# HGRN2's lower bounds of the second layer, formed by channels in the first layer and loaded back in one broadcast

## The chip, the cores and the metric

The program runs on one core of a Trainium2 chip. The metric is device time in microseconds (us), the median of several executions; lower is better. The engines are named as in the profile: PE is TensorE's matmul stream, PEld its weight loads, DVE is VectorE, ACT is ScalarE, POOL is GpSimd, SP is SyncE. SPq and ACTq are the DMA queues that SP and ACT feed.

## The reference

Two layers of a hybrid model over 256 tokens of width 1024. In each layer one projection feeds four mixers of 256 channels each: HGRN2, GLA, RWKV-7 and RetNet. Their outputs go together through an output projection, a residual and a layer norm (LN1). The first layer then has a dense FFN, the second a mixture of eight experts (MoE).

The part that matters here is HGRN2's forget gate. Its lower bound is a softmax over the layers of a 2 x 256 table, summed up and taken relative to the first layer. So it is 0 in layer 0, and in layer 1 it is one number per channel:

```python
lb_all = jnp.cumsum(jax.nn.softmax(hgrn_lb_logits, axis=0), axis=0)
lb_all = lb_all - lb_all[:1]
...
f = lb + (1.0 - lb) * jax.nn.sigmoid(f_raw)          # lb = lb_all[l]
o = _chunked_gated_linear(silu(q), 1.0 - f, i, log(f))
o = _rms_norm(o, norm_g) * silu(g)
```

## The kernel before, in words

Everything is float32. A weight tile is loaded by SP into one of three `raw` buffers. ACT rounds it to its high part (`wH`), DVE forms the rest (`wL`), and PE multiplies with three matmuls per product (line 146). Names that begin with `Pws` and `Pas` are the accumulators of the input projection, `XT` is the layer's input, `YT` the input of the output projection.

Each layer runs RWKV-7 first, then RetNet, HGRN2 and GLA (`ORDER` is "rhg"). The pieces of the input projection that the later mixers need are jobs: they are interleaved with the small matmuls of the mixers (`between`, line 308) so that PE has work while a mixer waits for DVE, ACT or POOL. A scheduler then sets the order of the instructions on each engine; each engine runs its own in that order. The y of HGRN2 and of GLA (`y_late`, line 729) is transposed inside the output projection, whose parts run in the order (6, 4, 0, 2), so those of HGRN2 and GLA are the last two. The layer norm's first matmuls are called `bank_o`.

HGRN2's chain in `hgrn` (lines 673 to 718) is: three activations of the gate's input (`hg_e`, `hg_s`, `hg_e`), the lower bounds, the product and the sum with them on `hg_e` (lines 702 and 703), the logarithm `hg_lf` (line 704), its split `hs_lfH` and `hs_lfL`, matmuls with constants (`Phs_ps`), exponentials `hg_E`, score matmuls (`Phs_p1p`), masked copies into `lin_S`, the output (`Ppo`), the norm and `y_late`. In layer 0 there are no lower bounds. In layer 1 both rows of the logits are loaded as broadcasts to all 128 partitions (`bcast`, line 393, on ACT's queue), and the softmax is computed on 128 x 256 tiles: the same 256 numbers on every partition (lines 686 to 701).

A second copy of the program (`general`) stands behind a branch at the end and is not taken with these inputs.

Of the kernel before, what the change touches and what calls it, by code (L numbers as in the profile page):

```python
# [9 lines left out]
F32 = mybir.dt.float32  # L10
# [3 lines left out]
AF = mybir.ActivationFunctionType  # L14
OP = mybir.AluOpType
# [109 lines left out]
class Build:  # L125
# [547 lines left out]
    def hgrn(self, l, xf, qT, V, G):  # L673
        nc, I, c, p = self.nc, self.I, self.c, self.mp
        xf = xf()
        e = self.t2([128, 2, 256], n="hg_e")
        s = self.t2([128, 2, 256], n="hg_s")
        self.act(e, xf, AF.Exp, scale=-1.0)
        self.act(s, e, AF.Ln, bias=1.0)
        self.act(e, s, AF.Exp, scale=-1.0)  # L680
        lf = self.t2([128, 2, 256], n="hg_lf")
        kt = self.t2([128, 2, 256], n="hg_kt")
        if l == 0:
            self.ts(lf, s, -1.0, None, OP.mult)
        else:
            b0 = self.bcast(self.t2([128, 256], n="hg_b0"), I["hgrn_lb_logits"][0])
            b1 = self.bcast(self.t2([128, 256], n="hg_b1"), I["hgrn_lb_logits"][1])
            m = self.t2([128, 256], n="hg_m")
            self.tt(m, b0, b1, OP.max)
            self.tt(b0, b0, m, OP.subtract)  # L690
            self.tt(b1, b1, m, OP.subtract)
            self.act(b0, b0, AF.Exp)
            self.act(b1, b1, AF.Exp)
            self.tt(m, b0, b1, OP.add)
            nc.vector.reciprocal(m, m)
            self.tt(b0, b0, m, OP.mult)
            self.tt(b1, b1, m, OP.mult)
            self.tt(b1, b0, b1, OP.add)
            self.tt(b1, b1, b0, OP.subtract)
            om = self.t2([128, 256], n="hg_om")  # L700
            self.ts(om, b1, -1.0, 1.0, OP.mult, OP.add)
            self.tt(e, e, om[:, None, :].to_broadcast([128, 2, 256]), OP.mult)
            self.tt(e, e, b1[:, None, :].to_broadcast([128, 2, 256]), OP.add)
            self.act(lf, e, AF.Ln)
        self.ts(kt, e, -0.5, 0.5, OP.mult, OP.add)
        kT = self.t2([128, 2, T], n="hg_kT")
        ps = self.mx("Phg_ps1")
        for a in range(2):
            for tt in range(2):
                self.tr(ps[:, a * 256 + tt * 128:a * 256 + tt * 128 + 128], kt[:, tt, a * 128:(a + 1) * 128], self.ident)  # L710
        self.act(kT, ps.rearrange("p (a t) -> p a t", a=2))
        o = self.t2([128, 2, 256], n="hg_o")
        if self.general:
            self.gated_linear(2, qT(), kT, lf, V(), o)
        else:
            self.hgrn_scores(l, qT, kT, lf, V, o)
        self.dump(f"hgrn_o{l}", o)
        self.gated_norm(o, I["hgrn_norm_g"][l], G(), 0)

    def gated_norm(self, o, g, G, ct):  # L720

        ng = self.bcast(self.t2([128, 64], n="gn_ng"), g)
        self.ts(ng, ng, 0.5, None, OP.mult, eng=self.nc.gpsimd)
        v = o.rearrange("p t (h v) -> p (t h) v", v=64)
        gv = G.rearrange("p t (h v) -> p (t h) v", v=64)
        self.tt(gv, gv, ng[:, None, :].to_broadcast([128, 8, 64]), OP.mult, self.nc.gpsimd)
        self.head_norm(v, 1e-6, False, "gn")
        if ct in LATE:
            o = self.lp.tile([128, 2, 256], F32, name="y_late")
        self.tt(o.rearrange("p t (h v) -> p (t h) v", v=64), v, gv, OP.mult)  # L730
        if ct in LATE:
            self.tails[ct] = lambda: self.put_y(o, ct)
        else:
            self.put_y(o, ct)
# [925 lines left out]
```

## Time and profile before

| | |
|---|---|
| median of 3 runs | 1102.84 us (1101.68 to 1105.39) |
| profiled execution, its own time | 1104.21 us |
| its span in the trace | 1102.7 us |
| mean granted clock of PE | 0.971 |
| PE busy | 1045.3 us (95%) |
| DVE busy | 792.8 us (72%) |
| ACT busy | 617.1 us (56%) |
| POOL busy | 67.5 us (6%) |

The profiled execution is 1.4 us above the median, and 1.5 us of it lie outside the span. Times of the trace are counted from the span's start. PE is busy nearly throughout, but the granted clock is below 1 in some stretches, and a matmul at the lower clock counts as busy for longer. So busy time alone does not tell what bounds a stage. Layer 0's mixers run from 0 to about 218 us, its FFN follows, layer 1's mixers end near 641 us, and the MoE fills the rest.

### The profile page before, as it was taken

How to read it: one execution, taken by the hardware profiler on the slowest of the kernel's cores; microseconds unless marked ns; L12 is line 12 of the kernel's file. 1: busy time of each engine (PE TensorE's matmuls, PEld its weight loads, DVE VectorE, ACT ScalarE, POOL GpSimd, SP SyncE). 2: the span in 40 equal slices, each digit the busy share in tenths (PEclk: the TensorE clock that was granted, in tenths of full speed). 3: DMA queues.
4: the chain of work that ended last, by engine and by line, in shares of the span. 5: the costliest groups of instructions: out<-in, count | busy, mean ns of one | idle time of the engine just before them, and what ended most of it. 6: DMA issues, size and time to landing. Idle time of an engine off the chain costs nothing. (4 is left out here: it accounts for less than half of the span.)

```text
span 1102.7 us, 17027 instructions
## 1 busy us (share of the span) xinstructions
PE 1045.3 (95%) x6664; PEld 906.6 (82%) x6664; DVE 792.8 (72%) x1171; ACT 617.1 (56%) x871; POOL 67.5 (6%) x92
## 2 busy tenths in 40 slices
PE   7799989999999999899899899999999999999995
PEld 6788878799999888888787677888888888877883
DVE  4584675565656456685673577998999899989986
ACT  4534264345555343633363435787788778777763
POOL 2000021100000002000102140000000000010001
PEclk9899998999999999999987999999999999999998
DMA  9244244336567363343151194998899889988952
GB/s 302 87 111 126 72 154 155 116 110 188 178 189 254 139 209 124 108 116 123 48 183 49 49 362 135 356 381 297 317 353 359 310 307 362 353 274 314 363 192 79
DMA packets 142161, 228.83 MB, mean 208 GB/s; under 512 B 17604, under 2 KB 89848, under 8 KB 142072
## 3 DMA queue, kind: packets, MB, share of 16 engines
q1 hardware_dynamic: 135104, 219.76, 58.4%
q10 hardware_dynamic: 6968, 7.90, 2.2%
q8 instruction: 54, 0.88, 0.3%
q14 instruction: 35, 0.29, 0.1%
HBM read 224.50 MB, written 3.15 MB: 206 GB/s over the span
## 5 line engine op out<-in xcount | busy, mean ns | idle before, releaser
L136 DVE TENSOR_TENSOR wL<-raw,wH 128x1024 fp32r<-128x1024 f32 (+2 forms) x477 | 501.6, 1065 | 164.6 <-ACT wH L133 157.8
L133 ACT ACTIVATE wH<-raw 128x1024 fp32r<-128x1024 f32 (+2 forms) x481 | 442.1, 927 | 272.5 <-PE Pws_ps L146 94.8
L146 PE MATMUL Pws_ps<-XT,wH 128*128 128x256 f32 (+1 forms) x1248 | 234.1, 288 | 9.1 <-DVE rc_x L143 8.3
L146 PE MATMUL Pms_ps<-wH,e_X 128*128 128x512 f32 (+1 forms) x768 | 226.9, 374 | 0.0
L146 PEld LDWEIGHTS Pws_ps<-XT,wH 128*128 128x128 f32 (+1 forms) x1248 | 196.4, 192 | 13.1 <-DVE rc_x L143 9.3
L146 PE MATMUL Pws_ps<-XT,wL 128*128 128x256 f32 (+1 forms) x624 | 178.3, 286 | 0.1
L146 PEld LDWEIGHTS Pms_ps<-wH,e_X 128*128 128x128 f32 x768 | 142.1, 188 | 20.2
L146 PE MATMUL Pms_ps<-wL,e_X 128*128 128x512 f32 (+1 forms) x384 | 144.1, 375 | 1.7 <-DVE wL L136 1.7
L146 PEld LDWEIGHTS Pws_ps<-XT,wL 128*128 128x128 f32 (+1 forms) x624 | 119.7, 192 | 1.1 <-issue 0.3
L146 PE MATMUL bank_dn<-wH,e_aT 128*128 128x512 f32 x352 | 112.9, 398 | 0.3
L146 PE MATMUL Pas_ps<-wH,XT 128*128 128x256 f32 x448 | 96.1, 302 | 4.6 <-ACT p_v L133 3.2
L146 PEld LDWEIGHTS Pas_ps<-wH,XT 128*128 128x128 f32 x448 | 75.8, 200 | 9.8 <-ACT p_v L133 4.5
L146 PEld LDWEIGHTS Pms_ps<-wL,e_X 128*128 128x128 f32 x384 | 72.2, 188 | 13.4 <-DVE wL L136 2.4
L146 PEld LDWEIGHTS bank_dn<-wH,e_aT 128*128 128x128 f32 x352 | 66.0, 188 | 17.2 <-DVE e_X L136 1.6
L146 PE MATMUL bank_dn<-wL,e_aT 128*128 128x512 f32 x176 | 69.8, 396 | 0.0
L146 PE MATMUL Pas_ps<-wL,XT 128*128 128x256 f32 x224 | 67.5, 302 | 0.6 <-DVE wL L136 0.5
L146 PEld LDWEIGHTS Pas_ps<-wL,XT 128*128 128x128 f32 x224 | 44.7, 200 | 3.9 <-DVE wL L136 2.4
L146 PEld LDWEIGHTS bank_dn<-wL,e_aT 128*128 128x128 f32 x176 | 33.1, 188 | 7.6
L146 PE MATMUL bank_acc<-wH,ffn_a 128*128 128x512 f32 x88 | 33.5, 394 | 0.0
L146 PE MATMUL bank_r<-wH,ffn_a 128*128 128x512 f32 x88 | 33.3, 392 | 0.0
L146 PE MATMUL bank_acc<-wH,YT 128*128 128x512 f32 x64 | 26.3, 446 | 1.2 <-ACT YT L133 1.2
L133 ACT ACT_TABLE_LOAD x19 | 24.4, 1283 | 1.6 <-PEq L1647 1.2
(385 smaller groups left out, 1238.1 us busy)
## 6 DMA issues: line engine op xcount, KB each, us to landing
raw<-in_moe_w_down SPq DMA_DIRECT2D x40, 1024.0 KB
raw<-in_moe_w_gate SPq DMA_DIRECT2D x32, 1024.0 KB
raw<-in_moe_w_up SPq DMA_DIRECT2D x32, 1024.0 KB
raw<-in_w_in SPq DMA_DIRECT2D x29, 1024.0 KB
raw<-in_moe_w_gate SPq DMA_DIRECT2D x16, 768.0 KB
raw<-in_moe_w_up SPq DMA_DIRECT2D x16, 768.0 KB
raw<-in_ffn_w_gate SPq DMA_DIRECT2D x11, 1024.0 KB
raw<-in_ffn_w_up SPq DMA_DIRECT2D x11, 1024.0 KB
```

The costliest lines, as they stand in the source:

```text
L133: return self.nc.scalar.activation(out=out, in_=in_, func=func, **k)
L136: return (eng or self.nc.vector).tensor_tensor(out=out, in0=a, in1=b, op=op)
L146: return self.nc.tensor.matmul(out=out, lhsT=lhsT, rhs=rhs, start=start, stop=stop)
```

## The change

The softmax moves to layer 0, into a new function that is called between HGRN2's scores and its norm. It works by channels: 256 channels lie as 128 partitions x 2, so a row of logits is a tile of 128 x 2. Two loads bring the logits (element by element), eight DVE operations and one ACT exponential of 2 or 4 elements per partition form `lb_x` (the bound, and 1 minus it), and two small DMAs on SP's queue write it to DRAM (`lbd`, 2 x 256). In layer 1 one broadcast load on ACT's queue brings both rows to all partitions (`hg_lb`). The product, the sum and the logarithm stay. The branch `general` keeps the old form.

```diff
@@ hgrn
         if l == 0:
             self.ts(lf, s, -1.0, None, OP.mult)
+        elif not self.general:
+            lb = self.t2([128, 2, 256], n="hg_lb")
+            nc.scalar.dma_start(lb, self.lbd.rearrange("(o x) c -> o x c", o=1).to_broadcast([128, 2, 256]))
+            b1, om = lb[:, 0, :], lb[:, 1, :]
+            self.tt(e, e, om[:, None, :].to_broadcast([128, 2, 256]), OP.mult)
+            self.tt(e, e, b1[:, None, :].to_broadcast([128, 2, 256]), OP.add)
+            self.act(lf, e, AF.Ln)
         else:
             b0 = self.bcast(self.t2([128, 256], n="hg_b0"), I["hgrn_lb_logits"][0])
...
         self.dump(f"hgrn_o{l}", o)
+        if l == 0 and not self.general:
+            self.lower_bounds()
         self.gated_norm(o, I["hgrn_norm_g"][l], G(), 0)
+
+    def lower_bounds(self):
+
+        nc, p = self.nc, self.lp
+        b, x, m = (p.tile([128, 2, 2], F32, name="lb_" + k) for k in "bxm")
+        for l in range(2):
+            nc.scalar.dma_start(b[:, l, :], self.I["hgrn_lb_logits"][l].rearrange("(a p) -> p a", p=128))
+        self.tt(m[:, 0], b[:, 0], b[:, 1], OP.max)
+        self.tt(b, b, m[:, 0:1].to_broadcast([128, 2, 2]), OP.subtract)
+        self.act(b, b, AF.Exp)
+        self.tt(m[:, 0], b[:, 0], b[:, 1], OP.add)
+        nc.vector.reciprocal(m[:, 0], m[:, 0])
+        self.tt(b, b, m[:, 0:1].to_broadcast([128, 2, 2]), OP.mult)
+        self.tt(m[:, 1], b[:, 0], b[:, 1], OP.add)
+        self.tt(x[:, 0], m[:, 1], b[:, 0], OP.subtract)
+        self.ts(x[:, 1], x[:, 0], -1.0, 1.0, OP.mult, OP.add)
+        self.lbd = self.dp.tile([2, 256], F32, name="lbd")
+        for i in range(2):
+            nc.sync.dma_start(self.lbd[i].rearrange("(a p) -> p a", p=128), x[:, i, :])
```

The scheduler moves instructions with it. Three places matter.

**DVE in layer 1, up to the sum on `hg_e`.** Before, the reciprocal, four more operations on the bounds and `hg_om` stand in front of the product, with pieces of weights (`wL`) between them (the rows begin at the reciprocal; the first `hg_m` is nine rows further up, right behind the row `YT<-Ppy_ps`):

```order
L695 RECIPROCAL hg_m<-hg_m 128x256
L143 SCALAR_TENSOR_TENSOR p_g<-p_g,Pas_ps_5886 128x256
L136 TENSOR_TENSOR hg_b_5785<-hg_b_5785,hg_m 128x256
L136 TENSOR_TENSOR hg_b_5787<-hg_b_5787,hg_m 128x256
L136 TENSOR_TENSOR wL<-raw,wH 128x768
L136 TENSOR_TENSOR hg_b_5787<-hg_b_5785,hg_b_5787 128x256
L136 TENSOR_TENSOR wL<-raw,wH 128x768
L136 TENSOR_TENSOR hg_b_5787<-hg_b_5787,hg_b_5785 128x256
L136 TENSOR_TENSOR wL<-raw,wH 128x512
L140 TENSOR_SCALAR hg_om<-hg_b_5787 128x256
L136 TENSOR_TENSOR hg_e<-hg_e,hg_om 128x512
L136 TENSOR_TENSOR hg_e<-hg_e,hg_b_5787 128x512
```

Now:

```order
L136 TENSOR_TENSOR YT<-Ppy_ps_5788,YT 128x2x256
L136 TENSOR_TENSOR rw_y<-rw_y,rw_W_5295 128x512
L136 TENSOR_TENSOR hg_e<-hg_e,hg_lb 128x512
L136 TENSOR_TENSOR wL<-raw,wH 128x768
L136 TENSOR_TENSOR YT<-rw_y,YT 128x2x256
L136 TENSOR_TENSOR hg_e<-hg_e,hg_lb 128x512
L136 TENSOR_TENSOR wL<-raw,wH 128x768
L140 TENSOR_SCALAR hg_kt<-hg_e 128x512
```

The product takes the place that the first `hg_m` had, and the sum stands one piece of weights and one `YT` behind it.

**ACT in layer 1, around the logarithm.** Before:

```order
L133 ACTIVATE p_g<-Pas_ps_5885 128x256
L133 ACTIVATE hg_b_5785<-hg_b_5785 128x256
L133 ACTIVATE hg_b_5787<-hg_b_5787 128x256
L133 ACTIVATE wH<-raw 128x512
L133 ACTIVATE p_g<-Pas_ps_5886 128x256
L133 ACTIVATE wH<-raw 128x768 x2
L133 ACTIVATE p_q<-Pws_ps_6017 128x256
L133 ACTIVATE wH<-raw 128x512
L133 ACTIVATE p_q<-Pws_ps_6018 128x256
L133 ACTIVATE wH<-raw 128x768
L133 ACT_TABLE_LOAD
L133 ACTIVATE hg_lf<-hg_e 128x512
```

Now:

```order
L133 ACTIVATE wH<-raw 128x768
L133 ACTIVATE p_g<-Pas_ps_5886 128x256
L133 ACT_TABLE_LOAD
L133 ACTIVATE hg_lf<-hg_e 128x512
L133 ACTIVATE hg_kT<-Phg_ps_5809 128x512
```

The logarithm follows directly on the first half of the gate `p_g`; the two exponentials are gone, and five pieces of weights, the gate's second half and `p_q` no longer stand in front of it.

**DVE in layer 0, early in RWKV-7.** Although the call is written behind HGRN2's scores, the scheduler puts the softmax where DVE waits for RWKV-7's `rw_rn`. Before, `rw_kk` followed directly on `wL<-raw,wH 128x512`. Now:

```order
L140 TENSOR_SCALAR rw_rn<-Prw_ps_376 128x512
L136 TENSOR_TENSOR wL<-raw,wH 128x512
L136 TENSOR_TENSOR lb_m<-lb_b 128x2
L136 TENSOR_TENSOR lb_b<-lb_b,lb_m 128x4
L136 TENSOR_TENSOR lb_m<-lb_b 128x2
L739 RECIPROCAL lb_m<-lb_m 128x2
L136 TENSOR_TENSOR lb_b<-lb_b,lb_m 128x4
L136 TENSOR_TENSOR lb_m<-lb_b 128x2
L143 SCALAR_TENSOR_TENSOR rw_kk<-rc_x,psmall,rw_rn 128x256 x2
L136 TENSOR_TENSOR lb_x<-lb_m,lb_b 128x2
```

Six small operations stand in front of `rw_kk` and a seventh behind it; the eighth comes six rows later. On ACT the exponential of `lb_b` stands directly in front of the exponential that ends `rw_rn`, and the two loads of logits go out right after `rw_lw` and after the second `wH` of 128x768 that follows. The two writes of `lbd` stand on SP behind the first ten loads of `w_in`, and the next load of `w_in` now comes ahead of RWKV-7's first write to DRAM instead of behind it. Layer 1's PE rows behind GLA's gate matmuls (`Pga`) are now 70 rows of the input projection, where 5 stood before (66 in layer 0).

## Rows read from the trace of the kernel before

**Rows 1.** Busy time by stretch; columns: stretch, length, busy by engine (instructions), PEclk, DMA, GB/s.
```profile
140.60:218.20 77.60, 73.53 (x465) 62.15 (x465) 47.53 (x88) 39.12 (x79) 13.59 (x16) 0.93 0.43 148
551.60:640.70 89.10, 81.95 (x474) 68.86 (x474) 49.47 (x94) 42.32 (x82) 12.12 (x17) 0.85 0.35 115
588.90:607.00 18.10, 18.02 (x76) 14.68 (x76) 4.97 (x14) 6.62 (x17) 4.21 (x4) 0.57 0.18 61
772.00:872.00 100.00, 99.83 (x486) 83.92 (x485) 91.17 (x98) 76.61 (x88) 0.00 (x0) 1.00 0.93 332
```

**Rows 2.** PE's waits from 551.6 to 640.7: total, times, longest (us).
```profile
PE Ppy_ps L149 <- DVE y_late L136: 2.3, 1, 2.3
...
PE bank_acc L146 <- ACT YT L133: 1.2, 1, 1.2
```

**Rows 3.** Timeline of DVE, layer 1: start, length, instruction, [idle before <- releaser].
```profile
556.04 0.42 DVE L136 TENSOR_TENSOR hg_m<-hg_b,hg_b 128x256 f32<-128x256 f32 x1
557.68 0.96 DVE L136 TENSOR_TENSOR wL<-raw,wH 128x768 fp32r<-128x768 f32 x1 [1.23 <-ACT wH L133]
558.56 0.68 DVE L136 TENSOR_TENSOR YT<-rw_y,YT 128x512 fp32r<-128x512 f32 x1
...
561.97 1.75 DVE L695 RECIPROCAL hg_m<-hg_m 128x256 f32<-128x256 f32 x1
...
567.91 0.69 DVE L136 TENSOR_TENSOR hg_e<-hg_e,hg_om 128x512 f32<-128x512 f32 x1
568.63 0.69 DVE L136 TENSOR_TENSOR hg_e<-hg_e,hg_b 128x512 f32<-128x512 f32 x1
...
606.79 0.69 DVE L136 TENSOR_TENSOR hg_o<-hg_o,hn_rs 128x512 f32<-128x512 f32 x1 [2.91 <-POOL hn_rs L136]
...
631.46 0.68 DVE L136 TENSOR_TENSOR y_late<-ga_o,p_g 128x512 f32<-128x512 f32 x1
```

**Rows 4.** Timeline of ACT, layer 1 (ACTq: its DMA queue).
```profile
545.72 0.35 ACTq L393 DMA_DIRECT2D hg_b<-in_hgrn_lb_logits  x1
...
559.10 0.39 ACT L133 ACTIVATE p_g<-Pas_ps 128x256 f32<-128x256 f32 x1
...
569.67 1.28 ACT L133 ACT_TABLE_LOAD   x1
570.97 0.63 ACT L133 ACTIVATE hg_lf<-hg_e 128x512 f32<-128x512 f32 x1
...
572.26 0.62 ACT L133 ACTIVATE hs_lfH<-hg_lf 128x512 fp32r<-128x512 f32 x1
```

**Rows 5.** Timeline of ACT, layer 0: the same split of the logarithm.
```profile
147.71 0.62 ACT L133 ACTIVATE hs_lfH<-hg_lf 128x512 fp32r<-128x512 f32 x1
```

**Rows 6.** Waits of SP's queue from 540 to 700: total, times, longest.
```profile
SPq L1544 <- DVE y_late L136: 41.3, 1, 41.3
```

**Rows 7.** Timeline of SP's queue, layer 1.
```profile
562.08 28.79 SPq L334 DMA_DIRECT2D raw<-in_w_out  x4
```

**Rows 8.** Timeline of all engines, layer 0, 29 to 46.
```profile
29.44 0.60 ACT L133 ACTIVATE rw_lw<-Prw_ps 128x512 f32<-128x512 f32 x1 [4.44 <-DMA rw_g<-in_rwkv_g]
...
34.97 0.23 ACTq L852 DMA_DIRECT2D gla_w<-in_gla_gate_b  x1
...
41.68 0.72 ACT L133 ACTIVATE rw_rn<-rw_rn,rw_b 128x512 f32<-128x512 f32 x1
...
42.44 0.88 DVE L143 SCALAR_TENSOR_TENSOR rw_kk<-rc_x,psmall,rw_rn 128x256 f32<-128x256 f32 x2 [3.29 <-ACT rw_rn L133]
...
45.70 0.80 PE L146 MATMUL Pws_ps<-XT,wH 128*128 128x256 f32 x2 [4.52 <-DVE rc_x L143]
```

**Rows 9.** Timeline of DVE, layer 0: two small operations, the second on the first's result.
```profile
141.17 0.17 DVE L140 TENSOR_SCALAR hn_s<-hn_s 128x8 f32<-128x8 f32 x1
141.38 0.17 DVE L140 TENSOR_SCALAR rs_ve<-hn_s 128x8 f32<-128x8 f32 x1
```

**Rows 10.** Timeline around the router's load, layer 1.
```profile
627.98 0.46 ACTq L1382 DMA_DIRECT2D e_rt<-in_moe_router  x1
...
630.33 0.26 ACT L133 ACTIVATE e_rHL<-e_rt 128x64 fp32r<-128x64 f32 x1 [2.58 <-DMA e_rt<-in_moe_router]
```

**Rows 11.** Timeline of SP's queue, layer 0.
```profile
26.20 13.35 SPq L230 DMA_DIRECT2D raw<-in_w_in  x2
55.28 0.34 SPq L1085 DMA_DIRECT2D rw_d<-rw_AT  x1
```

## The prediction

> **What bounds the kernel now.** I read the busy time by stretch first, because the change touches two stages out of many and shares of the whole span would hide both. From 772 to 872, in the MoE, PE is busy for 99.83 of 100 us at full clock [rows 1]: nothing that DVE or ACT saves there counts, and what happens ahead of the MoE passes to the end of the program whole, if the MoE's own start moves with it. It does: its weight loads wait on SP for `y_late` for 41.3 us [rows 6], so they follow the end of layer 1's mixers.
>
> The stage to read is therefore the one from RWKV-7's last transposes to the first matmuls of LN1. In layer 1 it takes 89.10 us, in layer 0, where HGRN2 has no lower bounds, the same stage with nearly the same matmuls (465 and 474 records) takes 77.60 [rows 1]. Look at where the 11.5 us lie. PE's busy time differs by 8.4 us, but it is counted at a granted clock of 0.85 against 0.93, and the stretch from 588.9 to 607.0 runs at 0.57, close to the lower of the two levels. PE idles 7.15 us in layer 1's stage, mostly on results of the mixers, the longest late one on `y_late` (2.3 us) [rows 2].
>
> Next, the timelines of DVE and ACT show what is late. In layer 0 the logarithm's split `hs_lfH` starts at 147.71, which is 7.1 us into the stage [rows 5]; in layer 1 at 572.26, 20.7 us into it [rows 4]. The reader is to see that the lower bounds lie in between: `hg_m` at 556.04, the reciprocal of 1.75 us at 561.97, the product at 567.91, the sum at 568.63 [rows 3], a table load of 1.28 us and the logarithm from 570.97 to 571.60 [rows 4]. These operations are short, yet each stands in its turn behind pieces of weights; the chain pays the queue, not only the work.
>
> **Removed, in layer 1.** Eight 128 x 256 operations of about 0.42 us and the reciprocal of 1.75 [rows 3]: 5.1 us of DVE, with `hg_om` on top, and two exponentials on ACT. As plain DVE time they would be worth little, since DVE is busy for 49.5 of 89.1 us [rows 1]. They count by what they hold back. In the new order the product takes `hg_m`'s place at 556.04; its 0.69 us push nothing, because DVE waits 1.23 us for `wH` before 557.68 [rows 3]. The sum stands behind one `wL` and one `YT`, so it runs at 559.2 and ends near 559.9. ACT ends the first half of `p_g` at 559.5 [rows 4], then loads the table (1.28) and runs the logarithm (0.63): `hg_lf` ends at 561.4 instead of 571.6. **HGRN2's chain starts 10.2 us earlier.** The broadcast load goes out at about 545.7, where the first of its two predecessors did [rows 4], and is needed at 556: 10 us for one load of the kind that had landed there before.
>
> **What the stage makes of 10.2 us.** From `hs_lfH` to the end of the stage it took 68.4 us in layer 1 (572.26 to 640.70) and 70.5 in layer 0 (147.71 to 218.20) [rows 1, 4, 5]. With `hs_lfH` now at 562.1, the stage would end between 630.5 and 632.6: 8.1 to 10.2 us are gained. Above that lies what the clock may give back. PE now gets 65 more projection rows to stand behind the gate matmuls, as in layer 0, so the half-clock stretch may shrink; it costs at most 18.1 x (1 - 0.57) = 7.8 us, and with the idle 7.15 that is 15 us, the most that the stage can give. Below, nothing is gained if the output projection's loads decide instead. I take 10.0, near the upper of the two templates, since layer 1's own distance holds its own waits and layer 0's order was planned with another set of loads.
>
> **Added, in layer 0.** The softmax lands in front of `rw_kk`, at a place where DVE waits 3.29 us for ACT's `rw_rn` [rows 8], so the first two small operations and the writes cost nothing. Then the exponential of `lb_b` stands in front of the one that ends `rw_rn` at 41.68 [rows 8]; the nearest row is 0.26 us for 128 x 64 [rows 10]. Four dependent small operations follow on DVE at steps of 0.21 us, as two operations of 8 elements show [rows 9]: 41.94 + 0.84 = 42.78, against 42.44 for `rw_kk` before. With one more 0.21 behind it, `rc_x`, on which PE waits 4.52 us until 45.70 [rows 8], is about 0.6 us later. PE's new order and a reordered load there may cost up to 2 us or give 1 back: SP's load of `w_in` now goes ahead of the write at 55.28 [rows 11]. I take 0.6, with 0 and 2.5 as ends. Without that cover, all nine operations would cost some 2 us. The `lbd` writes go out near 46, when SP is waiting for that write anyway, and are read 500 us later: nothing.
>
> The loads of logits are the one unknown. They go out near 30.0 and 35.0, and the first is needed only so that ACT's exponential can start at 41.7, some 6 us after the second. No row has a load of single elements. The nearest, the router's 1024 runs of 8 numbers, went out at 627.98 and had landed at 630.33, 2.35 us later [rows 10]; the far end is RWKV-7's load `rw_g`, for which ACT waited 4.44 us among the first weights [rows 8]. Either is hidden, so I take nothing. The Trainium skill speaks against this form: "DMA: Bandwidth & Descriptors", Rules for kernel authors, says that a last dimension that isn't contiguous becomes one descriptor per element, and Specifications that transfers under 512 bytes are read-modify-writes. By that rule each load is 256 descriptors and would be late; by the row it costs nothing; no run here has shown such a load yet. That case is the third rival.
>
> **Sum.** -10.0 + 0.6 = -9.4 us. The profiled execution took 1104.2, so 1094.8; it lay 1.4 above the median of 1102.84, which gives **1093.4 us** beside the median. The forecast's own range is 1090.6 to 1097.2: a gain of 10.2 and a quarter of the 7.8 us of clock with no cost in layer 0 at the one end, a gain of 8.1 with a cost of 2.5 at the other.
>
> **Rivals.**
>
> *1. Half is given back.* The pieces of weights that no longer stand in front of the logarithm have to stand somewhere. In DVE's new order two of 0.96 us and one of 0.68 come in front of the first masked copy of the scores, and one stands near the norm, where `hg_o` already waits 2.91 us for POOL's power [rows 3]. Then 10.2 - 2.6 - 2.9 - 0.6 leaves 4.1 us: 1098.7. For it: PE is in order, and score matmuls that come early wait in front of projections. Against: layer 0 has the same pile-up and still needs only 70.5 us.
>
> *2. The load hides it.* The four loads of `w_out` go out from 562.08 to 590.87, each when a `raw` buffer comes free [rows 7]. The change frees none earlier, and 65 more projection rows stand in front of the output projection. If these loads set its end, LN1 stays where it is, and only the cost in layer 0 remains: 1102 to 1104. Against: PE then waits for `y_late` and `YT` (2.3 and 1.2 us) and for no weights [rows 2].
>
> *3. Slower: the logits come late.* ACT is in order. If the second load takes longer than some 6 us, ACT stands at `lb_b`'s exponential with `rw_rn` behind it, DVE stands at `rw_kk`, PE at `rc_x`, and each us more passes to the end. At 4 us per such load (rows 8's wait) nothing happens; from 16 us on the gain is gone, and at 20 us the kernel is at 1093.4 + 14 = 1107. For it: only the rule just named. Against: 2.35 us for four times the runs [rows 10].
>
> *4. More than forecast.* The half-clock stretch goes and the waits with it: a gain of 13 to 15, 1088.4 to 1090.4.
>
> **Chances.** Forecast 0.62, rival 1 0.20, rival 2 0.10, rival 3 0.03, rival 4 0.05. Within 0.3% (3.3 us, about what a measurement of this kernel can tell from no change) lie 1099.5 to 1106.1: rival 2 and the slow edge of rival 1, 0.12. Slower is rival 3, 0.03. Faster: 0.85. The range takes in the forecast, most of rival 1 and part of rival 4: 1089.0 to 1100.0.
>
> **What would show it.** In the new profile: `hg_lf` ending about 10 us after the start of RWKV-7's last transposes instead of 20; the product on `hg_e` in front of the `wL` that waits for `wH`; the stage to `bank_o` near 79 us; the clock of the stretch behind the scores above 0.57; `rw_kk` at 42.8 in layer 0 with no DMA wait in front of `lb_b`; the MoE as before. The forecast is wrong if the logarithm is early and `bank_o` is not (rival 1 or 2: then PE's or SP's longest wait in the stage names which), or if ACT waits for `lb_b` on a DMA (rival 3).

## The result, and the profile after

The change made the kernel slower: 1111.42 us median of 9 runs against 1102.58 of 9 runs of the kernel before, a ratio of 1.0068 (95% interval 1.0042 to 1.0095). Forecast were 1093.4 us and 85% for faster; the range ended at 1100.0. The prediction was wrong in sign.

| | before | after |
|---|---|---|
| profiled execution, its own time | 1104.21 us | 1113.57 us |
| its span | 1102.7 us | 1111.0 us |
| mean granted clock of PE | 0.971 | 0.961 |
| PE busy | 1045.3 us | 1057.4 us |
| DVE busy | 792.8 us | 790.6 us |
| layer 0: first `bank_o` at | 218.22 | 219.46 |
| layer 1: last transposes of RWKV-7 at | 551.62 | 556.63 |
| layer 1: first `bank_o` at | 640.75 | 648.86 |
| from there to the end of the span | 462.0 us | 462.1 us |

The last line says where to look: from LN1 of layer 1 on nothing changed. Of the 8.3 us by which the span grew, 5.0 were there when layer 1's stage began, and 3.1 came in that stage. Only 1.2 of the 5.0 stand at layer 0's first `bank_o`. The other 3.8 come between it and layer 1's stage (333.4 us before, 337.2 after), and they are chance and not the change: a second profile of the kernel before takes 335.5 us for that stretch (e13), a second one of the change 335.6 (e1), and one with the change's layer 0 takes 333.5 (e4). Another 1.1 us lies outside the span (1.5 before, 2.6 after).

**The logarithm did come early.** ACT and DVE of the kernel after in layer 1, from the timelines:

```profile
561.52 0.68 DVE L136 TENSOR_TENSOR hg_e<-hg_e,hg_lb 128x512 f32<-128x512 f32 x1
562.48 0.96 DVE L136 TENSOR_TENSOR wL<-raw,wH 128x768 fp32r<-128x768 f32 x1 [0.28 <-ACT wH L133]
...
563.96 0.68 DVE L136 TENSOR_TENSOR hg_e<-hg_e,hg_lb 128x512 f32<-128x512 f32 x1
```

```profile
564.38 0.39 ACT L133 ACTIVATE p_g<-Pas_ps 128x256 f32<-128x256 f32 x1 [0.23 <-PE Pas_ps L146]
564.78 1.28 ACT L133 ACT_TABLE_LOAD   x1
566.08 0.63 ACT L133 ACTIVATE hg_lf<-hg_e 128x512 f32<-128x512 f32 x1
...
567.39 0.62 ACT L133 ACTIVATE hs_lfH<-hg_lf 128x512 fp32r<-128x512 f32 x1
```

The split `hs_lfH` stands 10.8 us into the stage (567.39 - 556.63), against 20.6 before [rows 4]: 9.8 us, where 10.2 were forecast. The product is in the place of the old `hg_m`, the table and the logarithm right behind `p_g`, as worked out.

**The stage still got longer.** By stretch, the kernel after (columns as in [rows 1]): the stage, a part of it behind HGRN2's scores, and the MoE.

```profile
556.63:648.86 92.23, 86.72 (x475) 73.94 (x475) 45.69 (x84) 42.69 (x81) 12.10 (x17) 0.80 0.36 123
590.00:605.00 15.00, 15.00 (x83) 14.03 (x82) 4.08 (x9) 5.16 (x15) 4.24 (x4) 0.66 0.02 4
780.00:880.00 100.00, 99.77 (x486) 83.88 (x485) 91.09 (x98) 76.62 (x88) 0.00 (x0) 1.00 0.94 331
```

92.2 us instead of 89.1 [rows 1], although DVE has 3.8 us less to do there. PE idles less (5.5 us against 7.15), but the clock went from 0.85 to 0.80. PE's timeline shows a first place where the 9.8 us went:

```profile
598.34 1.22 PE L146 MATMUL Pga_ps<-gla_w,glr 17*128 17x128 f32 x4
...
610.67 1.02 PE L146 MATMUL bank_acc<-h,alphaI 128*128 128x512 f32 x2
```

The same two rows of the kernel before:

```profile
601.56 1.22 PE L146 MATMUL Pga_ps<-gla_w,glr 17*128 17x128 f32 x4
...
603.95 1.91 PE L146 MATMUL bank_acc<-h,alphaI 128*128 128x512 f32 x2
```

Counted from each stage's start, GLA's gate matmuls come at 41.7 us instead of 49.9, so 8.2 of the 9.8 us arrive there. The first matmul of the output projection comes at 54.0 instead of 52.3: all gone. Between the two rows now stand the 70 rows of the input projection (12.3 us, against 2.4). Before, those rows had filled PE's time while HGRN2's chain was late. PE, busy for 92% of the stage before, had little idle time that an earlier chain could fill, and the rows only changed places.

**A new wait at the end of the stage.** What an early chain could still save lies later, between the two transposes of `y_late` and `bank_o`. From the timelines of SP's queue, ACT's queue, ACT and PE of the kernel after:

```profile
634.51 0.92 SPq L1572 DMA_DIRECT2D raw<-in_moe_w_gate  x2
...
635.01 0.45 ACTq L1410 DMA_DIRECT2D e_rt<-in_moe_router  x1
...
643.52 0.26 ACT L133 ACTIVATE e_rHL<-e_rt 128x64 fp32r<-128x64 f32 x1 [8.75 <-DMA e_rt<-in_moe_router]
643.68 0.58 ACT L133 ACTIVATE YT<-Ppy_ps 128x512 fp32r<-128x512 f32 x1
...
644.32 0.50 PE L146 MATMUL bank_acc<-wH,YT 128*128 128x512 f32 x1 [3.73 <-ACT YT L133]
```

Before, the router's load went out 4.3 us ahead of the MoE's first weight load (627.98 [rows 10]; SP's row is below) and landed in 2.35 us.

```profile
632.28 1.21 SPq L1544 DMA_DIRECT2D raw<-in_moe_w_gate  x2
```

Now it goes out 0.5 us behind those loads and takes 8.5 us. ACT takes its instructions in order: it stands at `e_rHL`, the second `YT` behind it, and PE behind `YT` for 3.73 us. The wait costs more than its own length, since the clock is lower behind it. The last 4.56 us ahead of `bank_o`, in the kernel after and then in e4, where the wait is gone (columns as in [rows 1]):

```profile
644.30:648.86 4.56, 4.54 (x13) 3.32 (x13) 2.28 (x3) 4.56 (x5) 0.00 (x0) 0.63 1.03 387
```

```profile
632.84:637.40 4.56, 4.56 (x21) 3.51 (x19) 1.98 (x3) 2.96 (x3) 0.24 (x1) 1.00 1.10 353
```

**Layer 0.** The small operations took what was worked out. From the timeline of ACT and DVE in the kernel after:

```profile
29.72 0.41 ACTq L734 DMA_DIRECT2D lb_b<-in_hgrn_lb_logits  x1
31.75 0.39 ACTq L734 DMA_DIRECT2D lb_b<-in_hgrn_lb_logits  x1
...
36.41 0.15 DVE L136 TENSOR_TENSOR lb_m<-lb_b 128x2 f32<-128x2 f32 x1
...
39.02 0.20 ACT L133 ACTIVATE lb_b<-lb_b 128x4 f32<-128x4 f32 x1
...
39.26 0.16 DVE L136 TENSOR_TENSOR lb_m<-lb_b 128x2 f32<-128x2 f32 x1 [2.50 <-ACT lb_b L133]
39.46 0.17 DVE L739 RECIPROCAL lb_m<-lb_m 128x2 f32<-128x2 f32 x1
39.66 0.16 DVE L136 TENSOR_TENSOR lb_b<-lb_b,lb_m 128x4 f32<-128x4 f32 x1
39.85 0.16 DVE L136 TENSOR_TENSOR lb_m<-lb_b 128x2 f32<-128x2 f32 x1
39.93 0.88 DVE L143 SCALAR_TENSOR_TENSOR rw_kk<-rc_x,psmall,rw_rn 128x256 f32<-128x256 f32 x2
```

There is no DMA wait, and the steps are of 0.20 us. `rw_kk` starts at 39.93, not at 42.8 as worked out: `rw_rn` itself came earlier on ACT. What cost time there is PE's order. The kernel after, behind its wait for `rc_x`:

```profile
43.19 0.79 PE L146 MATMUL Pws_ps<-XT,wH 128*128 128x256 f32 x2 [4.66 <-DVE rc_x L143]
...
45.83 2.07 PE L146 MATMUL Prw_pss<-rw_AR,rw_BK 64*128 64x128 f32 x8
...
48.34 2.07 PE L146 MATMUL Prw_pss<-rw_AR,rw_BK 64*128 64x128 f32 x8
...
51.92 2.07 PE L146 MATMUL Prw_pss<-rw_AR,rw_BK 64*128 64x128 f32 x8
...
55.50 2.07 PE L146 MATMUL Prw_pss<-rw_AR,rw_BK 64*128 64x128 f32 x8
...
67.67 1.03 PE L146 MATMUL Prt_ps<-p_q,c_swap 128*128 128x256 f32 x4
```

The kernel before, from its 45.70 [rows 8] on:

```profile
49.69 1.71 PE L146 MATMUL Prw_pss<-rw_AR,rw_BK 64*128 64x128 f32 x16
...
51.88 1.71 PE L146 MATMUL Prw_pss<-rw_AR,rw_BK 64*128 64x128 f32 x16
...
62.07 1.03 PE L146 MATMUL Prt_ps<-p_q,c_swap 128*128 128x256 f32 x4
```

`rc_x` came earlier too (43.19). But the scheduler, planning with two loads more on ACT's queue, gave PE another order: RWKV-7's scores `Prw_pss` now start 2.6 us behind the idle time instead of 4.0, in pieces of 8 between projection rows. A piece of 8 takes 2.07 us, 16 took 1.71. From `Pws_ps` to `Prt_ps` it is 24.5 us instead of 16.4. The stretches behind the idle time in the kernel after, and then in the kernel before:

```profile
43.20:61.50 18.30, 18.30 (x76) 16.50 (x77) 9.06 (x15) 4.09 (x9) 0.00 (x0) 0.51 0.24 66
61.50:75.00 13.50, 12.58 (x101) 12.07 (x101) 11.83 (x30) 6.80 (x10) 0.00 (x0) 1.00 0.22 39
```

```profile
45.70:48.70 3.00, 3.00 (x14) 3.00 (x15) 2.93 (x6) 2.31 (x5) 0.00 (x0) 0.51 0.00 0
48.70:75.00 26.30, 24.35 (x196) 22.73 (x195) 23.24 (x60) 11.52 (x19) 0.10 (x1) 1.00 0.40 106
```

PE is busy without a gap in both first rows, at a granted clock of 0.51, which is the lower level of 1.2 GHz. It stays there for 18.3 us after the change and for 3.0 before; if all of its work there takes twice as long at half speed, the 15.3 us more cost some 7.6, an estimate beside the 8.1 us from `Pws_ps` to `Prt_ps`. For the runs below, the mean clock from 50 to 75 tells which of the two orders a profile shows: 0.78 after, 1.00 before.

### The profile page after: what moved, and what is told of

It reads as the page before. It is cut to its first block, busy times and chain, and to the rows that moved or that the text cites. A ratio compares the mean times of both kernels' runs of the same rounds, so it can differ in the third digit from the quotient of the medians.

```text
span 1111.0 us, 17026 instructions
## 1 busy us (share of the span) xinstructions
PE 1057.4 (95%) x6664; PEld 918.4 (83%) x6664; DVE 790.6 (71%) x1169; ACT 615.7 (55%) x870; POOL 67.6 (6%) x92
## 5 line engine op out<-in xcount | busy, mean ns | idle before, releaser
L146 PE MATMUL Pws_ps<-XT,wH 128*128 128x256 f32 (+1 forms) x1248 | 237.0, 289 | 9.2 <-DVE rc_x L143 8.5
L146 PEld LDWEIGHTS Pms_ps<-wH,e_X 128*128 128x128 f32 x768 | 142.1, 188 | 20.6
```

The lines of the kernel that those rows point to most:

```text
L146: return self.nc.tensor.matmul(out=out, lhsT=lhsT, rhs=rhs, start=start, stop=stop)
```

## Experiments

Four theories stood against each other. **A**: the router's load collides with the MoE's weights, and `YT` stands behind it on ACT. **B**: the early logarithm puts HGRN2's small matmuls where they lower the clock, and the gain is lost there. **C**: the softmax operations in front of `rw_kk` hold RWKV-7 of layer 0 back. **D**: not the operations, but the order of PE that comes with the early loads costs layer 0 its clock. Each time is the median of 6 to 12 runs, except that of e13, a single run. Medians of one chip are compared with the runs of before on that chip.

### e1_again: the change repeated

No edit.

> The changed kernel once more, for a second profile and the clock of each run. Theory A (a collision: ACT waits 8.75 us for the router's load, which now goes out behind the MoE's weight loads, and the last YT stands behind it, so PE waits 3.7 us): every profile shows this wait of PE, and the kernel is 3 to 9 us slower than before. Theory B (the clock: with the logarithm early, HGRN2's small matmuls are split from the projections, and PE spends about 10 us more at half clock): times follow the mean granted clock, near 1105 us at 0.970 and near 1112 at 0.961, and at equal clock the kernel is no slower than before. Theory C (the softmax in layer 0 delays PE there): the start of layer 1's mixers is 2 us or more later than before in this profile too.

Measured: 1109.26 us, ratio 1.0066 (1.0034 to 1.0098); waits as in the first profile of the change (PE for `YT` 3.6 us), clock from 50 to 75 0.77. The slowdown is reproduced. What A, B and C expected is all met: the wait is there, layer 1's stage starts at 558.63 us, 7.0 later than before, and the mean clock is 0.008 lower, which at 0.83 us per 0.001 (last section) is 6.6 us, about the whole loss. So this run does not tell the theories apart.

### e2_layer0_only: softmax in layer 0, layer 1 as before

```diff
-        elif not self.general:
-            lb = self.t2([128, 2, 256], n="hg_lb")
...
-            self.act(lf, e, AF.Ln)
```

> The softmax in layer 0 and its two writes as in the change, but layer 1 computes its bounds in the old way. Theory C: 2.5 us or more slower than before (1105 or more). Theories A and B: within 1.5 us of before, 1101 to 1104.

Measured: 1106.17 us, ratio 1.0025 (0.9998 to 1.0051), clock from 50 to 75 0.68; in layer 1 the short waits of before (`YT` 1.2 us). That is what C (and later D) expects, 2.6 us for layer 0's part by itself, but the interval just takes in no change.

### e3_layer1_only and e15_layer1_again: layer 1 changed, no softmax

The softmax is left out; the bounds are 512 numbers of a table of constants.

```diff
-            nc.scalar.dma_start(lb, self.lbd.rearrange("(o x) c -> o x c", o=1).to_broadcast([128, 2, 256]))
+            o = COFF["ret"][0] + 512
+            nc.scalar.dma_start(lb, I["cst"][0:1, o:o + 512].rearrange("o (x c) -> o x c", x=2).to_broadcast([128, 2, 256]))
...
-        if l == 0 and not self.general:
-            self.lower_bounds()
```

> No softmax at all: layer 1 loads its two rows in one broadcast from a block of constants with values between 0.01 and 0.125, all else in layer 1 as in the change. Left out: the lower bounds, so the values differ and the work behind them is the same. Theories A and B: slower than before by 3 to 9 us (1106 to 1112), with PE's wait for YT near 3.7 us. Theory C: faster than before by 5 us or more.

> The run with layer 1 alone, repeated beside the one below. If the program decides the clock of GLA's output (Ppo_ps) at about 612, the 24 matmuls take 2.9 us again and the time is 1105 again. If the clock there is chance, the time of this kernel and of the next lie together, within 3 us of each other, and in one of the two profiles or in both the same 24 matmuls take more than 5 us.

Measured: 1105.09 us (1104.44 without one run of 5623 us, whose cause isn't known) and 1105.81, ratios 1.0012 (0.9981 to 1.0044) and 1.0028 (0.9997 to 1.0059). Layer 0 is as before (clock 1.00 and 0.99 from 50 to 75), PE waits 3.6 us for `YT` in both. So the early logarithm, with the collision, gains nothing: C's 5 us are not there, and the loss is smaller than the 3 to 9 us that A and B expected of e3. Of e15's two branches neither fits in full: the 24 matmuls take 5.29 us this time, so the program alone does not decide the clock there, but e16 stands 4.5 us away and not within 3.

### e4_router_pool, e7_before_pool: the router's split taken off ACT

In the change, and in the kernel before:

```diff
-        self.split(self.rHL[:, :, 0:NE], self.rHL[:, :, 32:40], rt)
+        nc.gpsimd.tensor_copy(self.rHL[:, :, 0:NE], rt)
+        self.tt(self.rHL[:, :, 32:40], rt, self.rHL[:, :, 0:NE].bitcast(F32), OP.subtract, nc.gpsimd)
```

> The change, with the split of the router's weights moved from ACT and DVE to POOL, so that the last YT no longer stands behind the router's load. Theory A: PE's wait of 3.7 us in front of the last part of the output projection falls under 1 us, the half-clock stretch behind it goes, and the kernel is 5 to 7 us faster than the change, 1104 to 1106. Theory B: the wait goes, but the kernel gains less than 3 us, since the clock in the scores and outputs is as before.

> The kernel before, with the router's split on POOL. Theory A: before, the router's load goes out 4.3 us ahead of the MoE's weight loads and PE waits for y_late, not for this, so the edit is worth less than 1.5 us there: 1101 to 1104. If the edit is worth something by itself: 3 us or more faster than before.

Measured: 1103.54 us against 1109.26 for the change on the same chip (ratios to before 1.0027, 0.9999 to 1.0054, and 1.0066); the wait for `YT` is gone and the stage takes 83.2 us. In the kernel before the same edit does nothing: 1104.42 us, ratio 1.0006 (0.9981 to 1.0032). Both are as A says, each 0.4 or 0.5 us outside its range of absolute times.

### e5_held, e9_all_held, e10_all_held_pool: the softmax later in layer 0

e5 holds the softmax operations, e9 also the loads, e10 is e9 with the router on POOL.

```diff
+        with self.tc.issue_after(self.last_e):
             for l in range(2):
                 nc.scalar.dma_start(b[:, l, :], self.I["hgrn_lb_logits"][l].rearrange("(a p) -> p a", p=128))
...
+        with self.tc.issue_after(self.last_o), self.tc.issue_after(self.last_s):
             self.tt(m[:, 0], b[:, 0], b[:, 1], OP.max)
```

> The change, with the softmax's operations on DVE and ACT held back until HGRN2's scores in layer 0 are done; the two loads of logits stay early, and PE's order in RWKV-7 of layer 0 is that of the change. Theory D (order and clock in layer 0: RWKV-7's small matmuls now stand right behind PE's 4.5 us of idle time, and the clock stays at its lower level until about 61 us instead of 48): the clock from 50 to 75 stays near 0.77, and the kernel is within 2 us of the change, 1108 to 1112. Theory C (the softmax's operations in front of rw_kk): the clock there is back at 1.00 and the kernel is 3 to 5 us faster than the change.

> The change, with the two loads of logits held back as well, behind HGRN2's gate in layer 0, so that RWKV-7 of layer 0 has the order of before on every engine. Theory D: the clock from 50 to 75 is back at 1.00 and the kernel is 3 to 6 us faster than the change, 1104 to 1107; the wait of 3.6 us for YT in layer 1 stays. Chance (the runs merely fall on other clocks): clock and time as in the change.

> The kernel with everything held back, and the router's split on POOL besides. Theories A and D together: both losses are gone and layer 1's gain of about 6 us is left, 1095 to 1099, 4 to 8 us faster than before. If the early logarithm gains nothing in layer 1: within 2 us of before.

Measured: 1121.67 us (1.0159, 1.0110 to 1.0209), 1114.27 (1.0104, 1.0067 to 1.0141), 1109.43 (1.0069, 1.0045 to 1.0094). With the operations gone from `rw_kk` but the loads still early (e5) the clock from 50 to 75 stays at 0.72; with the loads held too (e9) it is 0.98. By the clock that is D and not C. The times missed what was expected of all three, so they decide nothing on layer 0: holding the softmax made a new wait in GLA of layer 0, 5.2 us in e9 and 5.5 in e5 (0.4 in both the kernel before and after), and layer 0's stage takes 86.9 to 90.2 us in the three, against 73.8 to 79.1 in all other profiles. It is the same kind of wait as the router's, ACT at a weight's load with `lin_S` behind it; ACT's and PE's rows in e9:

```profile
195.65 2.10 ACT L133 ACTIVATE wH<-raw 128x768 fp32r<-128x768 f32 x3 [7.17 <-DMA raw<-in_ffn_w_gate]
...
198.20 1.65 PE L146 MATMUL Pgs_ps<-gs_E 32*128 32x256 f32 x4 [5.22 <-ACT lin_S L133]
```

Between e9 and e10 the router on POOL is worth 4.8 us.

### e11_ffn, e16_ffn_again, e12_ffn_pool: the softmax inside the dense FFN

Loads at the FFN's seventh step, sums at its eleventh, so that layer 0's mixers keep their order on every engine; e12 also has the router on POOL.

```diff
+                if ft == 6 and not self.general:
+                    with self.tc.issue_after(sa):
+                        self.bound_loads()
+                if ft == 10 and not self.general:
+                    with self.tc.issue_after(sa), self.tc.issue_after(sv):
+                        self.lower_bounds()
```

> The softmax by channels and its way through DRAM stay, but they stand in the dense FFN of layer 0, where PE is busy throughout at full clock; layer 0's mixers then have the order of before on every engine, and layer 1 is that of the change. Theory D (the loss in layer 0 is one of order and clock): the clock from 50 to 75 is 1.00 and the kernel is 3 to 7 us faster than the change; theory A's wait of 3.6 us for YT stays, so it stands within 2 us of before, 1101 to 1105. If layer 1 alone is slower than before: 1106 or more.

> Softmax in the FFN, repeated. Its layer 1 has the order of the run above. If the program decides, 5.4 us for GLA's output again and 1111 to 1114; if it is chance, within 3 us of the run above.

> The same with the router's split on POOL. Theories A and D together: the wait for YT goes too, the stage from RWKV-7's last transposes to LN1 takes 83 us instead of 89, and the kernel is 4 to 7 us faster than before, 1096 to 1099. If the early logarithm is worth nothing: within 2 us of before.

Measured: 1113.57 us (1.0105, 1.0073 to 1.0138) and 1110.33 (1.0058, 1.0028 to 1.0087) with the collision; 1102.05 (1.0001, 0.9976 to 1.0025) without. The clock from 50 to 75 is 1.00. The collision is worth 11.5 us between e11 and e12. e11 and e16 are slower than D forecast, and e16 falls just below its own 1111 to 1114. e12's time is the one expected if the early logarithm is worth nothing, although its stage of layer 1 is the shortest of all (81.0 us); some of that is lost where the softmax now stands: layer 1's RWKV-7 begins (first `Prw_ps`) 223.0 to 224.3 us behind layer 0's first `bank_o` in these three profiles, 221.2 to 222.7 in the others.

### e13_before_again: the kernel before once more

No edit.

> The kernel before once more, for a second profile. Theory D: the clock from 50 to 75 is 1.00 again, and RWKV-7's rotation matmuls in layer 0 start within 17 us of the end of PE's wait. Chance: it falls below 0.85 here too.

Measured: 1095.64 us at a mean clock of 0.980. The clock from 50 to 75 is 0.98 and the rotation matmuls (`Prt_ps`) start 16.6 us after the wait, as D says. The stage of layer 1 takes 83.3 us instead of 89.1, with the same order, and the clock from 590 to 620 is 1.00. So a single profile of a stage carries some 6 us of chance, and the clock of 0.57 in [rows 1] was no fixed property of that order.

### e14_layer1_pool: layer 1 changed, no softmax, router on POOL

e3 with the edit of e4.

> No softmax at all, layer 1 as in the change, and the router's split on POOL. If the collision is all that keeps layer 1's early logarithm from paying (theory A), the wait of PE for the second YT (3.6 us in the run with layer 1 alone) goes and the time is 1096 to 1099. If what the logarithm gains is given to the clock in layer 1 whatever happens at the router (theory B), it is 1100 to 1104 with a mean clock below that of before.

Measured: 1099.62 us, ratio 0.9975 (0.9940 to 1.0009), 6.2 us below its neighbour with the collision (e15). It lies between what A (at most 1099) and B (at least 1100) expected, and the interval takes in no change. Its mean clock over all runs is that of before on its chip (0.9705 and 0.9707), so what the early logarithm loses in the change is the collision's and not B's. The router's load is as slow as in the change (621.46 to 629.99), but it is POOL that waits; from the timelines of ACT's queue and POOL:

```profile
621.46 0.45 ACTq L1409 DMA_DIRECT2D e_rt<-in_moe_router  x1
...
629.99 0.24 POOL L1413 CAST e_rHL<-e_rt 128x64 fp32r<-128x64 f32 x1 [4.72 <-DMA e_rt<-in_moe_router]
```

### The runs together

The stage of layer 1, from RWKV-7's last transposes to the first `bank_o`, in every profile, in us:

| order of layer 1 | profiles | mean |
|---|---|---|
| before (before, e13, e7, e2) | 89.1, 83.3, 88.2, 89.1 | 87.4 |
| early logarithm, collision (after, e1, e3, e15, e11, e16, e5, e9) | 92.2, 91.0, 88.6, 93.4, 94.2, 91.9, 93.5, 85.3 | 91.3 |
| early logarithm, no collision (e14, e4, e12, e10) | 83.2, 83.2, 81.0, 82.3 | 82.4 |

The early logarithm by itself saves 5.0 us of the stage, and with the collision that it brings the stage is 8.9 longer. Not all of that is the two mechanisms. From the first transpose of `y_late` to `bank_o` the four profiles without the collision take 10.2 us each, the eight with it 15.6 to 16.7 (mean 16.0), the four of before 13.4 to 14.8 (mean 14.4). There, where the router's load goes out and PE waits for `y_late` and `YT`, lie 4.2 of the 5.0 us and 5.8 of the 8.9. The other 0.8 and 3.0 arise earlier, where the load is not yet issued and the same kernel takes 73.0 us in e3 and 76.8 in e15, so I count that part as chance. The first `bank_o` of layer 0 stands between 212.5 and 218.5 in the nine profiles with the old order there (before, e3, e7, e11 to e16), and between 219.5 and 223.0 in the four with that of the change (after, e1, e2, e4): means of 215.7 and 221.2, 5.5 us. The sum, -5.0 + 8.9 + 5.5 = 9.4 us, stands beside the 8.8 first measured (1111.42 - 1102.58); with 3.0 of the 8.9 due to chance, that close a fit is luck. The timed runs give smaller terms, with intervals of 3 to 4 us to either side: -2.9 for the logarithm alone (e14), +6.2 for the collision (e15 against e14; 4.8, 5.7 and 11.5 in the other three pairs), +2.6 for layer 0 (e2). They sum to 5.9, beside 5.7 for the change repeated on e2's chip (e1). The signs and the order of size agree; the sizes are known to some 3 us, and only the collision's is clear of no change by timing alone.

## Why the prediction was wrong

**What bounds the kernel**: right in part. The MoE passed what came ahead of it whole (462.0 and 462.1 us). But the reading of the stage took late results of DVE and ACT for its limit, when PE was busy 81.95 of 89.10 us.

**Removed, in layer 1**: right. 9.8 us earlier against 10.2; `hg_lb` goes out at 550.90 and nothing waits for it at 561.52.

**What the stage makes of 10.2 us**: the step that failed. It took the distance from `hs_lfH` to the end as given, 68.4 us in layer 1 or 70.5 in layer 0, and chose a gain near the former. With the collision the distance is 81.5 (567.39 to 648.86). Without it, it is 72.6 in e14 (557.12 to 629.69) and 72.0 to 72.6 in e4, e10 and e12, longer than either template. Layer 1's own could not hold: its 68.4 us (63.5 to 68.6 in the four profiles of that order) belong to an order in which the 65 rows stand ahead of GLA's gate and cover HGRN2's chain. The text named these rows and counted them as a gain for the clock; that their own time would stand in front of the output projection was not in the sum. That these rows are the reason is read from the profiles; no run moved them alone. The other part is the reference: 89.1 us was the upper end of the stage before (83.3 to 89.1), so its half clock was counted as something that the change could win back.

**The collision was missed**, a wait of 3.73 us that the sum did not hold, in a sentence that was right: the MoE's loads follow `y_late` [rows 6]. [Rows 10] had the router's load landing in 2.35 us, and the prediction used that row only as a price for the logits. It did not ask whether the load would still be ahead of the MoE's once ACT's rows were reordered, nor who is behind it on ACT. DVE's second `y_late` now follows the first transposes directly, so SP's wait ends before ACT issues the load.

**Added, in layer 0**: the operations were priced well (steps of 0.20 against 0.21, and `rc_x` earlier instead of 0.6 later) and PE's new order was not. The cost was put at 0.6 with 2.5 as its end; it was 2.6 timed and 5.5 in the profiles. It was treated as a shift of a few rows, when the question was which rows come first behind PE's idle time.

**The loads of logits, and rival 3**: they were hidden. The second load, issued at 31.75 (not near 35.0, as the prediction had it), was used at 36.41 with no DMA wait, and the broadcast load in layer 1 had landed too. The Trainium skill, "DMA: Bandwidth & Descriptors", Rules for kernel authors, speaks against such element-by-element loads; with 4.66 us of cover that rule decided nothing here. The kernel is slower by a mechanism that no rival named.

**The other rivals**: rival 1, half given back, comes nearest for the logarithm alone, 4.1 us worked out and 2.9 measured in e14, but by number only: it blamed pieces of weights on DVE, and it is PE's projection rows that stand in between. Rival 2 has the right place (the output projection comes no earlier) and the wrong cause: PE's own rows, not loads of `w_out`. Rival 4's clock did not come back: 0.66 from 590 to 605, and 0.80 instead of 0.85 over the stage.

**What would show it**: the early `hg_lf` and the product ahead of `wL` came as told. The stretch behind the scores is above 0.57 (0.66), as the text asked, but the stage's clock fell, and the stage of 79 us did not come. The text's own test, an early logarithm with a late `bank_o`, is what happened, and the longest new wait, PE for `YT`, named the collision as it said it would.

**Open**: why 1.1 us more lie outside the span (e14, without the softmax, has 1.8); and why e11 and e16 take 4.5 us or more longer than e15 with the same order in layer 1, though the intervals of e15 and e16 overlap. In their profiles 1.8 and 3.1 us of it lie ahead of layer 1's RWKV-7, where the softmax stands, and 1.6 and 1.8 behind LN1 of layer 1. No version beat the kernel before beyond its interval: e12 computes everything and is equal; e14, the fastest, has no softmax.

## What to carry over

An early result is worth only what the next engine in the chain can do with it: where PE is 92% busy, ask which rows filled the time that is now saved, and where they stand next. Whatever moves on an in-order engine, look at each load that it issues and at which bulk loads are released near it; a small load that had always gone out 4 us early can become the wait of the stage when it goes out 0.5 us late. And when a few tiny operations or loads are added under a list scheduler, compare PE's order behind its next idle time first: in the profiles that cost 5.5 us here, and the operations none that shows.

## What the hardware showed that was not expected

**One kernel, one place, either clock.** e3 and e15 are the same kernel. Behind the same wait the same 24 matmuls take 2.89 us in one profile and 5.29 in the other; e3 first, then e15:

```profile
611.34 0.92 PE L146 MATMUL Pgs_ps<-gs_E 32*128 32x256 f32 x4 [0.76 <-ACT lin_S L133]
612.18 2.89 PE L146 MATMUL Ppo_ps<-p_v,lin_S 128*128 128x64 f32 x24
```

```profile
609.25 0.92 PE L146 MATMUL Pgs_ps<-gs_E 32*128 32x256 f32 x4 [0.77 <-ACT lin_S L133]
610.10 5.29 PE L146 MATMUL Ppo_ps<-p_v,lin_S 128*128 128x64 f32 x24
```

The granted clock from 605 to 625 is 1.00 and 0.74: full speed in the one, and in the other the lower level for about half of the time. Over the 32 runs of the kernel before on e1's chip the time fell by 0.83 us per 0.001 of mean clock, from 1109.2 to 1095.6 us. The mean clock of the repeated change there (0.964) is below that of before (0.972). That a lower clock goes with the loss is thus right in theory B, but not its cause: the places shown are RWKV-7 of layer 0 and the matmuls behind the wait for `YT`, 0.63 after the change against 1.00 in e4.

**What comes first behind an idle time.** After waits of 4.5 and 4.7 us for `rc_x`, projection rows had PE back at full clock 3.0 us later; with RWKV-7's small matmuls, in pieces of 8, between the first projection rows it stayed at 1.2 GHz for 18.3 us, busy without a gap. e1, e2, e4 and e5, which have that order, show it too (0.68 to 0.77 from 50 to 75), and the eleven profiles with the old order there do not (0.98 to 1.00).

**A small load among large ones.** The router's load was in use 2.3 to 2.5 us after its issue in the four profiles in which it goes out ahead of the MoE's loads (before, e2, e7, e13), and 8.2 to 8.6 us after it in the twelve in which it goes out 0.5 us behind them, whether ACT or POOL takes it.
